# Fourier folds moved into the last LRU head, gates cut up between channel-mixing blocks, output weights and decays placed elsewhere, and chunks of k one product later, in a two-layer diffusion trunk

## The chip, the cores and the metric

The kernel runs on one core of a Trainium2 chip. The metric is the device time of one execution in microseconds. The engines are TensorE (PE; its weight loads appear as PEld), VectorE (DVE), ScalarE (ACT), GpSimd (POOL) and SyncE (SP), which issues most of the DMAs. Each engine works through its own instructions in order and waits on semaphores.

## The reference

A trunk of two layers over 1024 latent tokens and 256 context tokens of width 1024. Each layer normalises its input, shifts and scales it by a modulation that is computed from a condition, mixes, normalises again and adds the result with a gate. Layer 0 mixes with eight RG-LRU heads and four Fourier groups, layer 1 with a bidirectional retention of four heads.

```python
def fourier_branch(z, w_f):
    zg = z.astype(jnp.float32).reshape(B_, T, FNET_GROUPS, FNET_GROUP_DIM)
    f = jnp.real(jnp.fft.fft2(zg, axes=(1, 3), norm='ortho'))
    y = jnp.einsum('btgi,gij->btgj', f, w_f.astype(jnp.float32))
...
def even_mixer(...):
    xa, xb, ga, gb = jnp.split(h @ w_in, cuts, axis=-1)
    ya, yca = rglru_branch(xa, xca, ...)
    yb = fourier_branch(xb, w_f)
    y = jnp.concatenate([ya * jax.nn.silu(ga), yb * jax.nn.silu(gb)], axis=-1) @ w_out
...
def reference(...):
    for layer in range(DEPTH):
        shift, scale, gate = ada_mod(c, mod_w[layer], mod_b[layer])
        h = rms_norm(x, pre_g[layer]) * (1.0 + scale[:, None]) + shift[:, None]
        y, yc = even_mixer(...) if layer % 2 == 0 else retention_mixer(...)
        x = x + gate[:, None] * rms_norm(y, post_g[layer])
```

## The kernel before

Each fp32 product is made of three matmuls on a high and a low part of both operands (`acc3`); `split` makes the parts, the high one by a cast on ACT (or DVE), the low one by a subtraction on DVE or POOL (`low`). The 1280 tokens are worked on in chunks of 512, 512 and 256 columns. Weights pass through three raw slots of one tag, `wr`, in the pool `wp`; modulation weights (`modw`) and the DFT tables (`dr`) take the same slots.

Layer 0 runs through eight LRU heads. The head with n = 7 also makes the first Fourier inputs with `four_z(8)` and `four_z(9)` and the channel matrices of group 0. Then comes the loop over the Fourier groups g = 0 to 3. For each of the two inputs of a group the even and odd folds `ze`, `zc` are formed (by POOL for the first, by DVE for the second), combined, and split into `zx`, `zh`, `zl`. Then a gate `gate_b(2g)` is computed (24 steps of three matmuls, `pj`), then a modulation column, and then the channel mixing: six matmuls per block into `pa`, three of them with 128 contraction rows (`zh`, `zl`) and, in the even half, three with a single one (`zx`). The DFT over tokens follows (`dftmm`, tiles `pd`) for two halves ct of the group's channels, with the second gate ahead of ct = 1, and DVE and ACT combine the results into `y`, which goes to DRAM as yb_d. `mod_next` emits the column matmuls `mod_c` and the next 32-column matmuls `mod_a` of a modulation.

In group 3 the gate 7 (with the loop over k outermost, `kouter`) comes ahead of pa; then `wp` is released, and the LRU results ya_d are read back (`load_y`) while the group ends. `first_half` of the output projection then goes over the output blocks f with weights from `w1tile`; the retention's decays (`kd`, `qd`, `msk`) are computed by ACT and DVE just ahead of it, and `second_half` adds the Fourier half.

In layer 1 a `unit` makes seven (or, with the tokens as output, five) products of 24 or 48 matmuls (`pst`), and after each product takes one step of the generator `side`. For v and g that generator is `chunks_k`, which reads q and k back from DRAM (qk_d, written by the unit before), transposes k (`pkt`) and writes it out for the retention. Its two `load_qk` come at its second step and the first chunk at its third.

The order on each engine is made by a scheduler by priorities: code that is written earlier goes first, and `tc.high_priority(offset=...)` moves a piece ahead by an offset.

## Time and profile before

| | |
|---|---|
| median of three runs | 1951.94 us (1946.73 to 1958.4) |
| the profiled execution | 1954.47 us |
| its span, first to last instruction | 1952.7 us |
| mean granted TensorE clock | 0.976 |
| busy: PE, DVE, ACT, POOL | 1878.2, 1328.4, 866.8, 618.6 us |

The profile gives one execution. TensorE's granted clock has two levels, 1.00 (2.4 GHz) and 0.50 (1.2 GHz). A matmul row gives its start and its duration; as matmuls are pipelined, the pace is read from the steps between starts. The releaser in brackets is what ended the idle time ahead of a row.

### The profile page before, as it was taken

What the parts mean: (1) busy time and instruction counts of PE and PEld (TensorE: products, weight loads), DVE (VectorE), ACT (ScalarE), POOL (GpSimd) and SP (SyncE); (2) the same over time, 40 slices, a digit from 0 to 9 for tenths busy, and PEclk for the clock granted to TensorE, in tenths of its full rate; (3) what the DMA queues carried; (4) which work ended last, traced back from release to release, by engine and by line L of the source; (5) the groups of instructions that cost most, each with busy time, mean ns of one, the idle gap of its engine ahead of it and who ended that gap; (6) DMA issues with size and microseconds to landing.
All of it is one profiled execution on the core that took longest, in us unless ns stands there. A gap on an engine that the chain in (4) does not pass through costs nothing. (4 is left out here: it accounts for less than half of the span.)

```text
span 1952.7 us, 27667 instructions
## 1 busy us (share of the span) xinstructions
PE 1878.2 (96%) x10418; PEld 1578.5 (81%) x10418; DVE 1328.4 (68%) x1884; ACT 866.8 (44%) x1447; POOL 618.6 (32%) x407
## 2 busy tenths in 40 slices
PE   7999999989999899999999999999998899999997
PEld 3788888878888788888998889888896577777776
DVE  6777888742333434477678768777675887888987
ACT  5577676521222253256453332424333555454542
POOL 2411211312121241153245426253340334444544
PEclk8999999979889999999999999999999999999998
DMA  7222213213212262263872654737467555565434
GB/s 282 93 79 63 89 66 100 95 63 116 92 60 82 92 243 87 75 206 110 268 231 91 228 164 142 262 106 247 127 215 239 171 180 165 155 188 156 143 100 157
DMA packets 165110, 284.46 MB, mean 146 GB/s; under 512 B 14928, under 2 KB 94064, under 8 KB 163824
## 3 DMA queue, kind: packets, MB, share of 16 engines
q1 hardware_dynamic: 132224, 258.39, 41.1%
q10 hardware_dynamic: 32656, 24.26, 3.8%
q8 instruction: 82, 1.34, 0.3%
q14 instruction: 52, 0.43, 0.1%
q0 software_dynamic: 96, 0.04, 0.0%
HBM read 206.09 MB, written 76.55 MB: 145 GB/s over the span
## 5 line engine op out<-in xcount | busy, mean ns | idle before, releaser
L64 POOL TENSOR_TENSOR wl<-wr,wh 128x512 fp32r<-128x512 f32 (+1 forms) x80 | 153.8, 1923 | 421.4 <-ACT wh L70 396.7
L70 ACT CAST w<-wr 128x1024 fp32r<-128x1024 f32 x132 | 138.6, 1050 | 272.6 <-PE pst L59 205.3
L66 DVE TENSOR_TENSOR w<-wr,w 128x1024 fp32r<-128x1024 f32 x104 | 139.1, 1338 | 127.0 <-ACT w L70 127.0
L59 PE MATMUL pj<-xh,wl 128*128 128x512 f32 x512 | 203.0, 396 | 3.6 <-POOL wl L64 3.6
L59 PE MATMUL pj<-xh,wh 128*128 128x512 f32 x512 | 205.1, 402 | 1.0 <-ACT wh L70 0.6
L59 PE MATMUL pj<-xl,wh 128*128 128x512 f32 x512 | 202.8, 396 | 1.2 <-POOL xl L64 1.2
L59 PE MATMUL po<-xh,w 128*128 128x512 f32 x512 | 167.1, 398 | 0.0
L59 PE MATMUL pst<-xh,w 128*128 128x512 f32 x512 | 166.2, 398 | 0.5 <-DVE w L66 0.5
L64 POOL TENSOR_TENSOR w<-wr,w 128x1024 fp32r<-128x1024 f32 x28 | 70.7, 2524 | 184.3 <-ACT w L70 181.1
L59 PEld LDWEIGHTS pj<-xh,wl 128*128 128x128 f32 x512 | 97.0, 189 | 25.0 <-POOL wl L64 4.5
L59 PEld LDWEIGHTS pj<-xh,wh 128*128 128x128 f32 x512 | 96.8, 189 | 23.2 <-issue 1.4
L59 PEld LDWEIGHTS pst<-xh,w 128*128 128x128 f32 x512 | 95.9, 188 | 23.6 <-DVE w L66 1.0
L59 PEld LDWEIGHTS pj<-xl,wh 128*128 128x128 f32 x512 | 97.0, 189 | 22.1 <-POOL xl L64 2.1
L59 PEld LDWEIGHTS po<-xh,w 128*128 128x128 f32 x512 | 96.0, 188 | 22.5 <-issue 0.5
L70 ACT CAST wh<-wr 128x512 fp32r<-128x512 f32 (+1 forms) x80 | 63.4, 793 | 113.5 <-PE ph L59 49.2
L59 PE MATMUL po<-stp,qt 128*128 128x512 f32 x384 | 99.8, 404 | 7.0 <-DVE stp L66 3.4
L59 PE MATMUL pds<-vp,kh 128*128 128x512 f32 x288 | 92.5, 406 | 10.3 <-ACT kh L1152 5.5
L59 PE MATMUL po<-xl,w 128*128 128x512 f32 x256 | 101.3, 396 | 0.0
L59 PE MATMUL pst<-xl,w 128*128 128x512 f32 x256 | 101.0, 395 | 0.0
L59 PEld LDWEIGHTS po<-stp,qt 128*128 128x128 f32 x384 | 73.0, 192 | 28.5 <-DVE stp L66 6.1
L59 PE MATMUL pst<-w,xh 128*128 128x256 f32 x512 | 93.7, 285 | 0.0
L59 PE MATMUL pj<-xc,wh 128*128 128x256 f32 x512 | 91.4, 279 | 0.0
(315 smaller groups left out, 4800.8 us busy)
## 6 DMA issues: line engine op xcount, KB each, us to landing
wr<-in_w SPq DMA_DIRECT2D x72, 512.0 KB, 4.3
vp<-v_d SPq DMA_DIRECT2D x44, 512.0 KB, 4.6
wr<-in_win SPq DMA_DIRECT2D x32, 512.0 KB, 3.7
modw<-in_modw SPq DMA_DIRECT2D x32, 512.0 KB, 3.5
wr<-in_wout SPq DMA_DIRECT2D x32, 512.0 KB, 3.6
wr<-in_wout SPq DMA_DIRECT2D x56, 256.0 KB, 2.7
v_d<-st SPq DMA_DIRECT2D x48, 256.0 KB, 4.4
qt<-qs_d SPq DMA_DIRECT2D x32, 384.0 KB, 3.3
```

Of the source, the lines that this page charges most:

```text
L59: nc.tensor.matmul(o, lhsT=a, rhs=b, start=start, stop=stop)
L64: nc.gpsimd.tensor_tensor(out=o, in0=x, in1=hh, op=ALU.subtract)
L66: nc.vector.tensor_tensor(out=o, in0=x, in1=hh, op=ALU.subtract)
L70: nc.scalar.copy(h, x)
```

## The change

Six edits. (1) `mod_c`: both column matmuls first, then the reads by DVE. (2) The folds of group 0 are made in the LRU head 7, each right behind its `four_z`; the sums and casts that follow (`channel_folds`) are given a priority 40 earlier there; the DFT tables have buffers of their own (two raw ones) and a load behind the code of the head, and their high parts are cast by ACT. (3) A gate is a generator of steps, and `take` lets some of them run between two pa blocks: gate 1 in group 0, the second half of gate 2g in groups 1 and 2, gate 7 in group 3. (4) In group 3 the ya_d loads start when pa is done; the weights of the output blocks f = 0 and 1 are loaded into the tiles of the folds, and the two blocks (chunks 0 and 2) are multiplied ahead of the release of the Fourier pools (`po0`); `pd` of ct = 1 is put in the PSUM tag mm. (5) The decays become a generator that `second_half` advances. (6) `chunks_k` starts with one more empty step.

```diff
+OF0 = 40
...
             for i, part in enumerate(parts):
+                mm(c[:, 2 * i:2 * i + 2], r[:, i * P:(i + 1) * P], sel, True, True)
+            for i, part in enumerate(parts):
                 ci = c[:, 2 * i:2 * i + 2]
-                mm(ci, r[:, i * P:(i + 1) * P], sel, True, True)
                 if part == 0:
...
+    fo = pool("four_fold")
+
+    def fold(z, ct):
+
+        s2 = fo.tile([P, 2], F32, tag=f"zsp{ct}", name="zsp", bufs=1)
+        nc.vector.tensor_scalar(out=s2[:, 0:1], in0=z[:, 512:513], scalar1=1.0 / 32, scalar2=None, op0=ALU.mult)
+        nc.vector.tensor_scalar(out=s2[:, 1:2], in0=z[:, T + 129:T + 130], scalar1=1.0 / 16, scalar2=None, op0=ALU.mult)
+        t = [s2]
+        for e, op in ((0, ALU.add), (1, ALU.subtract)):
+            w = fo.tile([P, 512], F32, tag=f"ze{e}{ct}", name=f"ze{e}", bufs=1)
+            wc = fo.tile([P, P], F32, tag=f"zc{e}{ct}", name=f"zc{e}", bufs=1)
+            (nc.vector if ct else nc.gpsimd).tensor_tensor(out=w.rearrange("p (two n) -> p n two", two=2),
+                                    in0=z[:, 0:512].rearrange("p (n two) -> p n two", two=2),
+                                    in1=z[:, T:512:-1].rearrange("p (n two) -> p n two", two=2), op=op)
+            nc.vector.tensor_tensor(out=wc, in0=z[:, T + 1:T + 129], in1=z[:, NT + 1:T + 129:-1], op=op)
+            t += [w, wc]
+        return t
...
-            zf0 = four_z(8)
+            zz0 = [fold(four_z(8), 0)]
...
-        nga = gate_a(n + 1) if n < 7 else four_z(9)
+        if n < 7:
+            nga = gate_a(n + 1)
+        else:
+            zz0.append(fold(four_z(9), 1))
...
+    def channel_folds(zz, off):
+
+        with tc.high_priority(offset=off):
+            zx = [fq.tile([1, 512], F32R, tag=f"zx{p}", name=f"zx{p}") for p in "hl"]
+            split(zz[0][1][0:1, :], *zx)
+            zs = fq.tile([P, 2], F32, tag="zss", name="zss")
+            for i, (a, b) in enumerate(zip(*zz)):
+                if i == 0:
+                    nc.vector.tensor_tensor(out=zs, in0=a, in1=b, op=ALU.add)
+                else:
+                    nc.vector.tensor_tensor(out=b, in0=a, in1=b, op=ALU.add if i < 3 else ALU.subtract)
+                    if i > 2:
+                        nc.gpsimd.memset(b[0:1, :], 0.0)
+            zf = []
+            for e in range(2):
+                zh = fq.tile([P, 512], F32R, tag=f"zh{e}", name=f"zh{e}")
+                zl = fq.tile([P, 512], F32R, tag=f"zl{e}", name=f"zl{e}")
+                split(zz[1][1 + 2 * e], zh, zl)
+                zf.append((zz[1][2 + 2 * e], zh, zl))
+        return zx, zz[0][0][0:1, :], zz[0][2][0:1, :], zs, zf
...
-    dh = fc.tile([P, 2, 1028], F32R, name="dh")
-    dl = fc.tile([P, 2, 1028], F32R, name="dl")
-    COSE, COSO, SINE, SINO = (0, 258), (258, 256), (514, 256), (770, 258)
+    dr = [fc.tile([P, 514], F32, tag="dr", name="dr", bufs=2) for _ in range(4)]
+
+    dh = [[fc.tile([P, 514], F32R, name=f"dh{j}{b}") for b in range(2)] for j in range(2)]
+    dl = [[fc.tile([P, 514], F32R, name=f"dl{j}{b}") for b in range(2)] for j in range(2)]
...
+    def take(gen, n=99):
+        for _ in range(n):
+            if next(gen, 0) == 0:
+                return
...
+        def gen():
+            wh, wl = wtile(I["win"][24 + n], OW0)
+            if kouter:
+                os_ = [ps.tile([P, 512], F32, tag="mm", name="pj", bufs=4) for _ in CHUNKS]
+                for k in range(KT):
+                    for ci, (c0, cn) in enumerate(CHUNKS):
+                        acc3(os_[ci][:, :cn], wh[:, k, :], wl[:, k, :], *hx[k][ci], k == 0, k == KT - 1)
+                    yield
+            for ci, (c0, cn) in enumerate(CHUNKS):
+                if kouter:
+                    o = os_[ci]
+                else:
+                    o = ps.tile([P, 512], F32, tag="mm", name="pj", bufs=4)
+                    for k in range(KT):
+                        acc3(o[:, :cn], wh[:, k, :], wl[:, k, :], *hx[k][ci], k == 0, k == KT - 1)
+                        if k < KT - 1:
+                            yield
+                intab(nc.scalar.activation(sgb[:, c0:c0 + cn], o[:, :cn], AF.Silu))
+                yield
+
+        return sgb, gen()
...
-        for j in range(2):
-            for b in range(2):
-                s = slice(b * 514, (b + 1) * 514)
-                dr = wp.tile([P, 514], F32, tag="wr", name="dr", bufs=WRB)
-                nc.sync.dma_start(dr, I["dftc"][:, j, s])
-                split(dr, dh[:, j, s], dl[:, j, s], he="v", le="g")
-
+        for b in range(2):
+            for j in range(2):
+                raw = dr[2 * b + j]
+                nc.sync.dma_start(raw, I["dftc"][:, j, b * 514:(b + 1) * 514])
+                split(raw, dh[j][b], dl[j][b], le="g")
+
+    dft_tables()
...
+            zz = []
+            for ct in range(2):
                 z = four_z(8 + 2 * g + ct)
                 mod_next()
...
-        sgb = [gate_b(2 * g), None]
-        if not g:
-            dft_tables()
+                zz.append(fold(z, ct))
+        zx, zsx, zcx, zs, zf = channel_folds(zz, 0 if g else OF0)
+
+        sg0, gen = gate_b(2 * g)
+        take(gen, 99 if g in (0, 3) else 12)
         mod_next()
+        sgb = [sg0, None]
+        if g in (0, 3):
+            sgb[1], gen = gate_b(2 * g + 1, g == 3)
         side = iter(())
-        if g == 3:
-            sgb[1] = gate_b(7, True)
-            mod_flush()
-            wp.release()
-            lc = pool("l1c", side="right")
-            stg = pool("stage", side="right")
-            yx = [[None] * 3 for _ in range(KT)]
-            side = load_y(load_raw(ya_d, [0, 2]), yx, "g")
...
+                    take(gen, 1 if e or g == 3 else 2)
...
+        if g:
+            take(gen)
+        if g == 3:
+            mod_flush()
+            wp.release()
+            lc = pool("l1c", side="right")
+            stg = pool("stage", side="right")
+            yx = [[None] * 3 for _ in range(KT)]
+            side = load_y(load_raw(ya_d, [0, 2]), yx, "g")
+            next(side)
+
+            z = fz.tile([P, NT + 2], F32R, tag="z", name="w0", bufs=2)
+            parts = [[[fq.tile([P, 512], F32R, tag=f"z{p}{e}", name="w0") for p in "hl"] for e in range(2)],
+                     [[z[:, 512 * e:512 * (e + 1)], fz.tile([P, 512], F32R, tag=n, name="w0")] for e, n in enumerate(("cwh", "cwl"))]]
+            w0 = []
+            for f in range(2):
+                for e in range(2):
+                    raw = fo.tile([P, 512], F32, tag=f"ze{e}{f}", name="wr0", bufs=1)
+                    nc.sync.dma_start(raw, I["wout0"][f, 0, :, 4 * e:4 * e + 4, :].rearrange("p k m -> p (k m)"))
+                    split(raw, *parts[f][e], le="vg"[f])
+                w0.append(parts[f])
...
             if ct and g < 3:
-                sgb[1] = gate_b(2 * g + 1)
+                if g:
+                    sgb[1], gen = gate_b(2 * g + 1)
+                take(gen)
                 mod_next()
...
-                o = ps.tile([P, 512], F32, tag="aux", name="pd", bufs=4)
-                b0, bn = blk
+                o = ps.tile([P, 512], F32, tag="mm" if g == 3 and ct else "aux", name="pd", bufs=4)
...
+    po0 = [[], []]
+    for f in range(2):
+        for ci in (0, 2):
+            c0, cn = CHUNKS[ci]
+            o = ps.tile([P, 512], F32, tag="mm", name="po", bufs=4)
+            for k in range(KT):
+                acc3(o[:, :cn], *[w0[f][k // 4][p][:, k % 4 * P:(k % 4 + 1) * P] for p in range(2)], *yx[k][ci], k == 0, k == KT - 1)
+            po0[f].append((c0, cn, o))
...
+    def decays():
+
+        mskE = stage(512).rearrange("p (a n) -> p a n", n=P)
+        nc.sync.dma_start(mskE, I["mskE"])
+        nc.sync.dma_start(lg, I["lg"].partition_broadcast(P))
+        nc.sync.dma_start(kx, I["kx"])
...
-            for c0, cn, o in outproj0(f, 0, yx, chunks, f == KT - 1):
+            for c0, cn, o in outproj0(f, 0, yx, chunks, f == KT - 1) if f > 1 or 1 in chunks else po0[f]:
...
-    steps(second_half([0, 2]), 99)
+    dec = decays()
+    for _ in second_half([0, 2]):
+        next(dec, None)
+    steps(dec, 99)
...
     def chunks_k(h):
+        yield
         yield
         xs = [load_qk(h, 0), load_qk(h, 1)]
```

On SP, at the end of head 7 and the start of group 0 (`dr`: DFT tables, `wr`: weights of a gate, `modw`: modulation weights, `ya_d`: the store of an LRU head's result, `cd`: for the channel matrices). Before:

```order
L544 DMA dr<-in_dftc 128x514 [waits DMAHW7_49,DMAHW5_49,Pool_49]
L544 DMA dr<-in_dftc 128x514 [waits DMAHW1_49,PE_49]
L544 DMA dr<-in_dftc 128x514 [waits DMAHW2_49,PE_49]
L544 DMA dr<-in_dftc 128x514 [waits DMAHW7_49,Pool_49]
L175 DMA modw<-in_modw 128x1024 [waits DMAHW0_49,Pool_49]
L175 DMA modw<-in_modw 128x1024 [waits DMAHW1_49,Pool_49]
L242 DMA wr<-in_win 128x1024 [waits DMAHW6_49,DMAHW2_49,Pool_49]
L485 DMA ya_d<-sga 128x1280 [waits DVE_49]
```

After:

```order
L176 DMA modw<-in_modw 128x1024 [waits DMAHW7_49,DMAHW5_49,Pool_49]
L176 DMA modw<-in_modw 128x1024 [waits DMAHW1_49,PE_49]
L244 DMA wr<-in_win 128x1024 [waits DMAHW2_49,PE_49]
L176 DMA modw<-in_modw 128x1024 [waits DMAHW1_49,Pool_49]
L508 DMA ya_d<-sga 128x1280 [waits DVE_49]
L176 DMA modw<-in_modw 128x1024 [waits DMAHW7_49,DMAHW4_49,PE_49]
L390 DMA cd<-in_cd 128x512 [waits DMAHW0_49,PE_49]
L627 DMA dr<-in_dftc 128x514 x2
L627 DMA dr<-in_dftc 128x514 [waits DMAHW7_49,Pool_49]
L627 DMA dr<-in_dftc 128x514 [waits DMAHW2_49,DMAHW0_49,Pool_49]
```

The gate's load moved ahead of the last head's store, and the tables moved behind it and behind two more loads.

On TensorE, at the start of the channel mixing of group 1 (`pj`: steps of gate 2, `zxh` and `zxl`: the one-row parts). Before:

```order
L59 MATMUL pa<-cwh,zh_3950 128x256
L59 MATMUL pa<-cwl,zh_3950 128x256
L59 MATMUL pa<-cwh,zl_3951 128x256
L59 MATMUL pa<-cwh,zxh 128x256
L59 MATMUL pa<-cwl,zxh 128x256
L59 MATMUL pa<-cwh,zxl 128x256
L59 MATMUL pa<-cwh,zh_3950 128x256
L59 MATMUL pa<-cwl,zh_3950 128x256
L59 MATMUL pa<-cwh,zl_3951 128x256
L59 MATMUL pa<-cwh,zxh 128x256
L59 MATMUL pa<-cwl,zxh 128x256
L59 MATMUL pa<-cwh,zxl 128x256
```

After:

```order
L60 MATMUL pa<-cwh,zh_3959 128x256
L60 MATMUL pa<-cwl,zh_3959 128x256
L60 MATMUL pa<-cwh,zl_3960 128x256
L60 MATMUL pa<-cwh,zxh 128x256
L60 MATMUL pa<-cwl,zxh 128x256
L60 MATMUL pa<-cwh,zxl 128x256
L60 MATMUL pj<-xh_127,wh 128x512
L60 MATMUL pj<-xl_128,wh 128x512
L60 MATMUL pj<-xh_127,wl 128x512
L60 MATMUL pj<-xh_132,wh 128x512
L60 MATMUL pj<-xl_133,wh 128x512
L60 MATMUL pj<-xh_132,wl 128x512
```

Between two blocks of six pa matmuls there are now six of the gate.

On SP, in group 3 (`in_wout`: weights of the output projection, `in_win`: those of gate 7, `ya_d`, `yb_d`: LRU and Fourier results). Before, at the first reads of ya_d, and at the first loads of output weights:

```order
L242 DMA wr<-in_win 128x1024 [waits DMAHW3_49,Pool_49]
L509 DMA st<-ya_d 128x512 [waits DMAHW2_49,DMAHW6_49,PE_49,Pool_49]
L505 DMA st<-ya_d 128x2x256 [waits DMAHW0_49,PE_49]
L509 DMA st<-ya_d 128x512 x2
L505 DMA st<-ya_d 128x2x256
L509 DMA st<-ya_d 128x512 [waits DMAHW4_49]
L509 DMA st<-ya_d 128x512 [waits DMAHW5_49]
```

```order
L509 DMA st<-ya_d 128x512 [waits DMAHW2_49]
L705 DMA wr_5853<-in_wout 128x1024 [waits DMAHW3_49,DVE_49,PE_49]
L705 DMA wr_5923<-in_wout 128x1024 [waits DMAHW4_49,PE_49]
L724 DMA st<-in_mskE 128x512 [waits DMAHW5_49,Pool_49]
L726 DMA lg<-in_lg 128x8 [waits DMAHW6_49,DVE_49]
L728 DMA kx<-in_kx 128x8 [waits DMAHW7_49]
L682 DMA yb_d<-y 128x1280 [waits DMAHW0_49,DVE_49]
L705 DMA wr_6133<-in_wout 128x1024 [waits DMAHW4_49,DMAHW1_49,Pool_49]
L705 DMA wr_6191<-in_wout 128x1024 [waits DMAHW3_49,DMAHW2_49,DVE_49]
L682 DMA yb_d<-y 128x1280 [waits DVE_49]
```

After, at the same two places:

```order
L244 DMA wr<-in_win 128x1024 [waits DMAHW3_49,Pool_49]
L692 DMA wr_5568<-in_wout 128x512 [waits DVE_49]
L692 DMA wr_5572<-in_wout 128x512 [waits DMAHW0_49,DVE_49]
L692 DMA wr_5576<-in_wout 128x512 [waits DVE_49]
L692 DMA wr_5580<-in_wout 128x512 [waits DMAHW2_49,DVE_49]
L531 DMA st<-ya_d 128x512 [waits DMAHW5_49,PE_49]
L527 DMA st<-ya_d 128x2x256 [waits DMAHW4_49,PE_49,Pool_49]
L531 DMA st<-ya_d 128x512
```

```order
L755 DMA yb_d<-y 128x1280 [waits DMAHW7_49,DVE_49]
L531 DMA st<-ya_d 128x512 [waits DMAHW0_49,Pool_49]
L531 DMA st<-yb_d 128x512 [waits DMAHW1_49,Pool_49]
L527 DMA st<-yb_d 128x2x256 [waits DMAHW2_49]
L787 DMA wr_5956<-in_wout 128x1024 [waits DMAHW3_49,PE_49]
L787 DMA wr_6026<-in_wout 128x1024 [waits DMAHW4_49,PE_49]
```

The early weights, in four pieces, now stand ahead of the reads of ya_d, and the load of the next block's weights behind the second store to yb_d and the first reads of it.

## Rows read from the trace of the kernel before

**Rows 1.** The profile page: busy time, share of the span, instructions of each engine.
```profile
PE 1878.2 (96%) x10418; PEld 1578.5 (81%) x10418; DVE 1328.4 (68%) x1884; ACT 866.8 (44%) x1447; POOL 618.6 (32%) x407
```

**Rows 2.** Timeline of TensorE (start us, us, engine, line, operation): the same matmul at either clock.
```profile
379.67 0.39 PE L59 MATMUL pj<-xh,wh 128*128 128x512 f32 x1
...
382.42 0.39 PE L59 MATMUL pj<-xh,wh 128*128 128x512 f32 x1
...
396.90 0.63 PE L59 MATMUL pj<-xh,wh 128*128 128x512 f32 x1
...
398.18 0.63 PE L59 MATMUL pj<-xh,wh 128*128 128x512 f32 x1
```

**Rows 3.** The same timeline, TensorE's waits in Fourier group 0 (idle before, releaser in brackets).
```profile
389.09 0.50 PE L59 MATMUL pj<-xh,wh 128*128 128x512 f32 x1 [0.60 <-ACT wh L70]
...
392.17 0.50 PE L59 MATMUL pj<-xh,wl 128*128 128x512 f32 x1 [2.34 <-POOL wl L64]
395.88 0.58 PE L59 MATMUL pa<-cwh,zh 128*128 128x256 f32 x1 [3.21 <-ACT zh L70]
```

**Rows 4.** Timelines of SP, ScalarE and GpSimd (POOL) ahead of the same place.
```profile
354.80 18.07 SPq L544 DMA_DIRECT2D dr<-in_dftc  x4
...
384.43 0.33 SPq L242 DMA_DIRECT2D wr<-in_win  x1
387.31 0.33 SPq L485 DMA_DIRECT2D ya_d<-sga  x1
...
387.99 1.05 ACT L70 CAST wh<-wr 128x1024 fp32r<-128x1024 f32 x1 [13.93 <-DMA wr<-in_win]
...
392.08 2.55 POOL L564 TENSOR_TENSOR ze<-z 128x512 f32<-128x512 f32 x2
```

**Rows 5.** Stretches: us; busy (instructions) of PE, PEld, DVE, ACT, POOL; clock; DMA share; GB/s.
```profile
395.88:412.00 16.12, 16.12 (x52) 12.65 (x52) 5.01 (x11) 3.71 (x7) 0.66 (x2) 0.50 0.06 25
412.00:416.95 4.95, 4.95 (x22) 4.75 (x23) 1.67 (x5) 0.64 (x2) 0.00 (x0) 0.50 0.00 0
488.00:492.04 4.04, 4.04 (x24) 2.99 (x23) 0.84 (x2) 0.59 (x1) 0.00 (x0) 1.00 0.60 195
492.04:502.28 10.24, 10.24 (x36) 8.46 (x37) 2.30 (x5) 4.08 (x8) 2.36 (x1) 0.50 0.17 53
573.96:584.20 10.24, 10.24 (x41) 9.20 (x41) 3.03 (x7) 3.35 (x7) 2.38 (x1) 0.50 0.17 51
669.53:672.94 3.41, 3.41 (x17) 3.20 (x15) 2.32 (x5) 2.76 (x6) 2.56 (x2) 0.50 1.05 377
679.77:686.60 6.83, 4.03 (x17) 3.61 (x17) 6.29 (x16) 3.22 (x7) 2.31 (x2) 0.50 0.23 86
739.00:770.00 31.00, 31.00 (x177) 26.85 (x176) 15.54 (x29) 11.20 (x19) 5.15 (x2) 1.00 0.32 103
1098.68:1103.03 4.35, 4.35 (x20) 4.35 (x21) 4.35 (x7) 0.86 (x3) 0.62 (x1) 0.50 0.32 85
```

**Rows 6.** Timeline of TensorE, one-row matmuls; then TensorE's waits (total us, times, longest).
```profile
488.15 0.38 PE L59 MATMUL pa<-cwh,zxh 1*128 1x256 f32 x1
...
PE pkt L59 <- DMA st<-qk_d: 5.9, 3, 4.7
PE mod_c L59 <- DVE sh L187: 1.6, 3, 0.6
```

**Rows 7.** Timelines of TensorE, SP and POOL in the last Fourier group.
```profile
679.13 0.39 PE L59 MATMUL pd<-dh,ah 128*128 128x258 f32 x1 [2.19 <-DVE spe L655]
...
683.09 0.55 PE L59 MATMUL pd<-dh,ah 128*128 128x256 f32 x1 [2.80 <-DVE y L671]
...
663.36 0.38 SPq L505 DMA_DIRECT2D st<-ya_d  x1
...
676.48 3.98 POOL L64 TENSOR_TENSOR xl<-st,xh 128x512 fp32r<-128x512 f32 x3 [0.49 <-ACT xh L70]
```

**Rows 8.** Timeline of TensorE at the first chunk of k.
```profile
1098.68 1.20 PE L59 MATMUL pkt<-st 128*128 128x128 f32 x4 [4.74 <-DMA st<-qk_d]
```

More of the change, by code (lines that the diff above doesn't have):

```diff
@@ L486, in _build @@
         sga = nga
-    zs0 = [zf0, nga]
     if "ya" in dbg:
@@ L527, in _build, with ftile @@
     fp = pool("four_out")
-    fq = pool("four_in")
+    first = {}
+    def ftile(shape, dt, tag, bufs=1):
+        if tag in first:
+            return first.pop(tag)
+        return fp.tile(shape, dt, tag=tag, name=tag, bufs=bufs)
+    LOW = (("nb", 4, 2), ("ac0", 256, 1), ("ac1", 256, 1), ("y", NT, 1), ("spe", 258, 1), ("u", 256, 1), ("sqe", 256, 1), ("v", 256, 1))
+    first.update({n: fp.tile([P, w], F32, tag=n, name=n, bufs=b) for n, w, b in LOW})
+    first.update({f"a{p}{e}{par}": fp.tile([P, 2, 256], F32R, tag=f"a{p}{e}{par}", name=f"a{p}", bufs=1)
+                  for e in range(2) for par in range(2) for p in "hl"})
@@ L581, in _build @@
-        zf = []
-        for e in range(2):
-            zh = fq.tile([P, 512], F32R, tag=f"zh{e}", name=f"zh{e}")
-            zl = fq.tile([P, 512], F32R, tag=f"zl{e}", name=f"zl{e}")
-            split(zz[1][1 + 2 * e], zh, zl)
-            zf.append((zz[1][2 + 2 * e], zh, zl))
-        sgb = [gate_b(2 * g), None]
-        if not g:
-            dft_tables()
+                zz.append(fold(z, ct))
+        zx, zsx, zcx, zs, zf = channel_folds(zz, 0 if g else OF0)
+        sg0, gen = gate_b(2 * g)
@@ L611, in _build @@
                         acc3(pa[:, j, :], zx[0][:, s], zx[1][:, s], ch[0:1, 1, :], cl[0:1, 1, :], False, True)
-                ah = fp.tile([P, 2, 256], F32R, tag=f"ah{e}{par}", name="ah")
-                al = fp.tile([P, 2, 256], F32R, tag=f"al{e}{par}", name="al")
+                    take(gen, 1 if e or g == 3 else 2)
+                ah, al = [ftile([P, 2, 256], F32R, f"a{p}{e}{par}") for p in "hl"]
                 split(pa, ah, al)
                 A[e, par] = (ah, al)
-                next(side, None)
             pa = ps.tile([P, 2, 256], F32, tag="aux", name="pac", bufs=4)
@@ L629, in _build @@
             mm(pn[:, 0:2], cf[0:1, 1, cs], zsx, False, True)
-            nb = fp.tile([P, 4], F32, tag="nb", name="nb", bufs=2)
+            nb = ftile([P, 4], F32, "nb", 2)
             nc.vector.tensor_copy(nb[:, 0:2], pn[:, 0:2])
@@ L663, in _build @@
             nc.vector.tensor_tensor(out=x, in0=sqe, in1=qo[:, 0:256], op=ALU.subtract)
-            y = fp.tile([P, NT], F32, tag="y", name="y", bufs=1)
+            y = ftile([P, NT], F32, "y")
             L = TC
@@ L1104, in chunks_k @@
     def chunks_k(h):
+        yield
         yield
```

91 lines of the change are left out of this document (31 added, 60 removed).

## The prediction

> **What bounds the kernel now.** I read the shares of busy time first: TensorE is busy for 96% of the span [rows 1], so no other engine sets the time as a whole, and a change can win in only two ways, by closing a gap in which TensorE waits or by undoing a stretch in which its granted clock stands at the lower of its two levels (0.50, that is 1.2 instead of 2.4 GHz). To price the second I compared the same matmul at both levels [rows 2]: between 379.67 and 382.42 there are twelve 512-column matmuls, 0.229 us each; between 396.90 and 398.18 there are three, 0.427 us each. A busy microsecond at the lower level therefore does what 0.534 us do at the upper, and 0.466 us of it are lost. Then I went through TensorE's order for its waits and through the table by stretches for the clock. Four places have both, and the change touches them all: the first Fourier group (388 to 417 us), the pa blocks of groups 1 and 2 (from 492 and 574), the last group (669 to 687), and the first chunk of k (1094 to 1103).
>
> **Folds in the last LRU head (g = 0).** Now TensorE waits 0.60 us for the cast wh, 2.34 for POOL's wl and 3.21 for zh [rows 3], 6.15 together, and works on at the lower clock for 16.12 + 4.95 = 21.07 us [rows 5]; 21.07 x 0.466 = 9.8. The cause stands in the other queues [rows 4]: the four dr loads hold the weight slots and their issue takes 18.07 us, so gate 1's weights are issued only at 384.43, cast at 387.99, and POOL does their low part before the fold of z8, which starts at 392.08 although z8 is old. In the new order gate 1's load stands ahead of the tables, the folds stand on POOL ahead of that low part, and the casts of zh follow in the last head. All three waits lose their cause: ceiling 6.15 + 9.8 = 15.95.
> What is late next is the DFT tables. On SP their loads now stand behind the store of head 7's ya_d, which goes out at 387.31 [rows 4] when DVE has finished the head, and behind a modulation load. With two buffers, the second pair also waits for POOL's dl of the first. TensorE wants the first table after pa and 12 of gate 1's steps. The pa work is 16.12 x 0.534 = 8.6, less 0.9 for four gate matmuls that lie in it, so near 8; a step of three 512-column matmuls is 0.69, twelve are 8.2. From 388.5 that is 405. A load took 3.56 us from issue to cast (384.43 to 387.99 [rows 4]). Loads issued at about 390 give the first pair by 396, the second after ACT's cast and POOL's low part at 402 to 407. So the stall is between 0 and 3 us; I take 1.5, since the first pair has time and only the second is near. The casts now sit on ACT, which waits there in order; behind them are pa's ah casts, and that is the way in which late tables would hurt earlier than 405. Term: **-14.5**.
>
> **Half of gate 2g between pa blocks (g = 1, 2).** At 488 to 492.04 TensorE is busy for 4.04 of 4.04 us at the full clock, and then the clock falls for 10.24 us, all busy; at 573.96 the same [rows 5]. What TensorE did before is a run of pa blocks in which half of the matmuls have a single contraction row (1x256, [rows 6]); so the clock fell without any idle time, after work that uses one row of the array. In the new order two gate steps, six full matmuls, follow each block of the first kind (the order shows it), which brings these one-row matmuls from half of the time to a quarter or a third. The added cost is none: the same matmuls, one PSUM tile longer in use. Bounds: nothing gained, or both stretches, 2 x 10.24 x 0.466 = 9.5; I take the latter, as 12 gate steps also stand ahead of the modulation matmuls. Term: **-9.5**.
> The Trainium skill (TensorE: Matmul & The Clock Gate, section "Why this matters for your kernels") names idle gaps between bursts of matmuls as what makes the throughput drop in the middle of a kernel. By that rule alone nothing would be gained here, as there is no gap to close; the rows speak against it, since they show the fall with TensorE busy throughout, and by it the sum would be 9.5 us smaller (the second rival).
>
> **mod_c.** Both column matmuls before their reads: the wait on DVE's sh, 1.6 us in three places [rows 6], has no cause left; DVE and TensorE do the same work. Term: **-1.6**.
>
> **The last group (g = 3) and two early blocks.** Now there are gaps of 2.19 and 2.80 us at the second half's pd [rows 7], and 3.41 + 4.03 busy us at the lower clock [rows 5], 7.44 x 0.466 = 3.5; ceiling 8.5. The gate between pa blocks, pd tiles in the other PSUM tag (so that they don't wait for DVE's reads) and early weights for f = 0, 1 take away each cause. What is late next: the ya_d loads started at 663.36 [rows 7], when gate 7 was done and pa was still to come. Now gate 7 ends with pa, some 7 us later, so they start near 670. POOL's low parts take 3.98/3 = 1.33 us each [rows 7], eight of them 10.6, and two low parts of the early weights stand ahead. The last x low comes near 685 to 687, while TensorE reaches po0 at about 678 (an estimate: pa's end near 670, then twice 24 pd matmuls of half a 512-column one, 2.8 us, with their small ones) and needs one k in 0.7 us. That costs 2 to 3 us in small pieces. Next, the load of f = 2's weights now waits for TensorE's last pd and stands on SP behind the last y's store and the first loads of yb; 3.56 us to its cast and POOL's low part put it within 0 to 3 us of being late. So the term lies between -8.5 and +1 (all of this late and the clock falling once more); I take -5. Term: **-5**.
>
> **Decays.** The exponentials move to second_half, where ACT is busy for 11.20 of 31.00 us [rows 5], so ACT's idle time hides them; without that cover they would delay the acc copies that free PSUM, by at most their few us. Term: **0**.
>
> **Chunks of k.** Waits for the qk_d reload are 5.9 us in three places [rows 6], the longest 4.74 [rows 8], after it 4.35 us at the lower clock [rows 5], 2.0. One product of 48 matmuls of 256 columns at 0.115 (half of 0.229), 5.5 us, now stands in between, so the data that came at 1098.68 are there when they are asked for, at 1099.2. The reload of the third chunk moves behind one more weight load; it is wanted a product later too. The eight chunks still end within the last unit. Ceiling 7.9; I leave 0.5 for the bare margin. Term: **-7.4**.
>
> **Sum.** -14.5 - 9.5 - 1.6 - 5 - 7.4 = -38.0. The profiled run took 1954.47 us, so it would take 1916.5; the median of the runs shown, 1951.94, lies 2.5 lower, which gives **1914** for a median.
>
> **Rivals.**
> 1. *Late tables.* For: the slack in group 0 is a microsecond at most, on three queues. Against: the first pair has several. The second pair late by 4 us and a clock stretch as at 492 (4.8) cost some 9 more than the 1.5 taken: 1922. Chance 0.12.
> 2. *The clock falls at pa as before.* The order changes, but the thing that it is meant to change doesn't: the one-row matmuls still come in blocks. For: that the fall is tied to them is read from two places only. Against: with six full matmuls after each block there is no run left like the one ahead of 492. 1914 + 9.5 = 1923.5. Chance 0.12.
> 3. *The last group gives back its gain.* ya_d, xl and f = 2's weights late, a gap over 2 us and a fall as at 679.77: 5 to 6 us lost: 1920. For: the loads start 7 us later. Against: 8 us of early weights that wait for nothing. Chance 0.12.
> 4. *Slower than before: the mixture itself keeps the clock down.* At 395.88 to 412, pa mixed with gate matmuls, the clock stayed low throughout [rows 5]. If the clock stays down wherever pa blocks and gate steps alternate, the mixed stretches run low from end to end: four times 8 us of pa and 8.2 + 5.6 + 5.6 + 13.9 of gate steps, 65 us at full clock, cost 65 x 0.873 = 57 more, less 9.8 + 9.5 + 1.6 that are lost there already, against some 17 us of other gains: 36 - 17 = +19, 1971. It decides from about 44 of the 65 us at the lower clock (38 / 0.873). Against: the clock there had fallen in a gap of 3.21 us, and only four gate matmuls were mixed in. Chance 0.05.
> The forecast has 0.55; two of the first three together (1930 to 1938) 0.04.
>
> **The range.** From 1900 (all ceilings: 15.95 + 9.5 + 1.6 + 8.5 + 7.9 = 43.5, so 1908 for a median, and 1903 if it falls as low as the lowest run shown stands under its median, 5 us; 3 more for what the sum doesn't see) to 1934 (the first three rivals, half of what two of them together give, and the spread of the runs). A measurement can tell about 0.5% from no change, 10 us. All cases but the fourth rival gain more than that unless several terms fail together: faster 0.90, same 0.04, slower 0.06.
>
> **What would show it.** In the new profile: no TensorE wait for wh, wl or zh ahead of the first pa, and the clock at 1.00 from there to the end of group 0; a wait of pd for dl or dh there is the first rival. Clock 1.00 through the pa of groups 1 and 2, or a stretch of 10.24 us at 0.50 as before. No wait on sh. After the last pa, waits of po on xl or w show the third. No wait of pkt on the reload. I am wrong altogether if a wait opens that the old trace doesn't hold, most likely where TensorE now meets the tables or f = 2's weights.

## The result and the profile after

| | before | after |
|---|---|---|
| median | 1949.74 us (4 runs) | 1924.78 us (4 runs, 1919.62 to 1925.78) |
| ratio | | 0.9868, interval 0.9843 to 0.9894 |
| profiled execution | 1954.47 us | 1925.78 us |
| mean granted clock | 0.976 | 0.989 |

The change wins 25 us in the medians (1.3%) and 28.7 between the profiled executions, against 38.0 forecast for the latter. TensorE is busy 25.5 us less for the same 10418 matmuls [rows 1]. The page's busy line:

```profile
PE 1852.7 (96%) x10418; PEld 1558.6 (81%) x10418; DVE 1323.4 (69%) x1881; ACT 866.1 (45%) x1453; POOL 620.9 (32%) x408
```

TensorE's waits of the changed kernel from 380 to 700 us (total us, times, longest):

```profile
PE po L60 <- ACT w L71: 4.4, 1, 4.4
PE po L60 <- ACT sqe L732: 3.7, 1, 3.7
PE pj L60 <- POOL wl L65: 1.3, 1, 1.3
PE pd L60 <- DVE al L67: 1.2, 1, 1.2
PE po L60 <- POOL xl L65: 0.3, 1, 0.3
```

The waits of [rows 3] on wh and zh are gone, as are those of [rows 7] on spe and y; in their place po, the early blocks of the output projection, waits for sqe (ACT's copy of a `pd`; only then is the PSUM tile free) and then for f = 2's weights. The same columns as in [rows 5], group 0, groups 1 and 2, and the two stretches of the last group at the lower clock:

```profile
388.00:412.00 24.00, 22.80 (x146) 18.75 (x138) 10.05 (x21) 9.53 (x20) 5.20 (x6) 1.00 0.31 105
480.00:520.00 40.00, 40.00 (x252) 34.81 (x251) 17.13 (x39) 9.18 (x19) 8.93 (x5) 1.00 0.32 106
560.00:600.00 40.00, 40.00 (x242) 34.41 (x241) 14.97 (x31) 9.29 (x19) 7.56 (x4) 1.00 0.31 105
655.56:658.97 3.41, 3.22 (x8) 2.54 (x9) 3.41 (x6) 1.95 (x5) 3.41 (x3) 0.50 0.13 52
679.45:682.86 3.41, 3.41 (x10) 2.65 (x10) 1.99 (x2) 3.28 (x5) 1.90 (x1) 0.50 0.67 205
```

Where 492.04 and 573.96 of [rows 5] stood at 0.50, the clock is now 1.00. And far behind every edit, in the first unit of layer 1, a wait has opened that the old trace doesn't hold:

```profile
1020.28 1.22 PE L60 MATMUL pst<-xh,w 128*128 128x512 f32 x2 [5.64 <-DVE w L67]
```

To place the gain, each matmul of one trace was set against the same matmul of the other. What the time ahead of before grows by, stage by stage (profiled executions):

| place | forecast | measured |
|---|---|---|
| start to 380 us | | -0.1 |
| group 0 | -14.5 | -14.9 |
| mod_c | -1.6 | -1.1 |
| groups 1 and 2 | -9.5 | -10.7 |
| last group, early blocks | -5 | +3.7 |
| clock at 922 us (3.41 us at 0.50 before, none now) | | -1.5 |
| unit at 1014 us | | +7.7 |
| first chunk of k | -7.4 | -7.6 |
| behind it, to the end | | -4.2 |
| sum | -38.0 | -28.7 |

Two places miss, by 8.7 and 7.7 us; 7 us are won beyond the forecast, most of them in places that it didn't name. Two rows are less than they seem. The stretch at 922 us stands in the same place of the program again in experiments 2, 7, 8 and 10 (from 901.27 us in the second), so its 1.5 us are probably chance and no gain of the change. And the unit at 1014 us and the first chunk of k hang together: without the edit of `chunks_k` (experiment 2), 5.9 of the 7.6 us come at the first chunk all the same, because the wait at 1014 has by then made TensorE late.

Single executions differ by up to 6 us in the first 60 us alone, where TensorE's wait for modr is 4.7 to 5.6 us in most and 1.27, 0.23 or nothing in three, so the experiments are read by such stages and not by their total.

### The profile page after: what moved, and what is told of

Its sections match the earlier page's. It is cut to its first block, busy times and chain, and to the rows that moved or that the text cites. A ratio compares the mean times of both kernels' runs of the same rounds, so it can differ in the third digit from the quotient of the medians.

```text
span 1924.0 us, 27696 instructions
## 1 busy us (share of the span) xinstructions
PE 1852.7 (96%) x10418; PEld 1558.6 (81%) x10418; DVE 1323.4 (69%) x1881; ACT 866.1 (45%) x1453; POOL 620.9 (32%) x408
## 5 line engine op out<-in xcount | busy, mean ns | idle before, releaser
L71 ACT CAST w<-wr 128x1024 fp32r<-128x1024 f32 (+1 forms) x134 | 138.9, 1038 | 279.2 <-PE pst L60 211.7
L67 DVE TENSOR_TENSOR w<-wr,w 128x1024 fp32r<-128x1024 f32 (+1 forms) x105 | 142.2, 1355 | 134.1 <-ACT w L71 124.2
L65 POOL TENSOR_TENSOR w<-wr,w 128x1024 fp32r<-128x1024 f32 (+1 forms) x29 | 73.6, 2541 | 214.8 <-ACT w L71 211.5
L60 PE MATMUL pds<-vp,kh 128*128 128x512 f32 x288 | 93.7, 409 | 13.8 <-ACT kh L1241 10.7
L60 PE MATMUL pst<-t,w 128*128 128x512 f32 x368 | 91.6, 397 | 0.0
```

What stands on the lines that cost most here:

```text
L60: nc.tensor.matmul(o, lhsT=a, rhs=b, start=start, stop=stop)
L65: nc.gpsimd.tensor_tensor(out=o, in0=x, in1=hh, op=ALU.subtract)
L67: nc.vector.tensor_tensor(out=o, in0=x, in1=hh, op=ALU.subtract)
L71: nc.scalar.copy(h, x)
```

## The experiments

**1. The slots of the output weights.** `w1tile` deals out slots in the pools wa and wb in turn; the two early blocks leave out two calls, so all later weights sit two slots further. This run puts the turn back.

```diff
-    turn = [0, 0]
+    turn = [2, 0]
```

> The changed kernel, with the counter that picks the weight slots of w1tile started at 2 instead of 0; nothing else. Theory: the two early output blocks (po0) call w1tile twice less, so every later weight tile sits in the other pair of slots, and layer 1's first unit finds another slot free first; that put its weight low parts behind others on DVE and made the 5.65 us wait of pst on DVE w at 1014 with 6.8 us at the lower clock. Then this kernel shows no wait over 1 us there, and everything behind it comes 7 to 8 us earlier: near 1918 us in one run. Rival: the wait comes from the extra empty step of the chunks of k; then it stays at 5 to 6 us and the time stays near 1925.

1920.56 us. At 1014 us 7.75 us come back, and 1.8 are lost again at 1075 (`pst` waits 1.41 for DVE's w); by the end 5.2 remain. So the shifted slots made the new wait. How is seen on POOL and DVE. The changed kernel, POOL and then DVE:

```profile
1006.67 2.40 POOL L1136 TENSOR_TENSOR wr<-wr,wr 128x1024 f32<-128x1024 f32 x1 [11.96 <-PE pst L60]
1009.14 2.73 POOL L1137 TENSOR_TENSOR wr<-wr,wr 128x1024 f32<-128x1024 f32 x1
1011.83 3.38 POOL L1139 TENSOR_TENSOR wr<-wr,wr 128x1024 f32<-128x1024 f32 x1
...
1010.19 2.77 DVE L67 TENSOR_TENSOR w<-wr,w 128x1024 fp32r<-128x1024 f32 x1 [0.57 <-ACT w L71]
1012.88 2.88 DVE L67 TENSOR_TENSOR st<-st 128x512 fp32r<-128x512 f32 x1
...
1019.01 2.35 DVE L67 TENSOR_TENSOR w<-wr,w 128x1024 fp32r<-128x1024 f32 x2
```

The first experiment's DVE:

```profile
1007.42 1.23 DVE L67 TENSOR_TENSOR w<-wr,w 128x1024 fp32r<-128x1024 f32 x1 [0.33 <-ACT w L71]
```

With the shifted slots POOL adds up the weights of the next product early, while DVE makes low parts; a low part then takes 2.77 instead of 1.23 us, and the one that TensorE wants is reached only at 1019.01. Of the theory's 7 to 8 us behind it, 5.2 are left.

**2. Without the step in chunks_k.**

```diff
     def chunks_k(h):
         yield
-        yield
```

> The changed kernel without the extra empty step of the chunks of k. Theory (slots): the wait at 1014 stays, 5 to 6 us, and the stall of pkt on the reload of qk_d comes back, 4.7 us and 2 us of clock at the first chunk and about 1 us more at later ones: 7 to 8 us slower than the changed kernel, near 1933. Rival (the step made the wait at 1014): that wait is gone, the stall is back, and the time is about the same as the changed kernel, 1925.

1932.88 us. The wait at 1014 stays (5.67), so the step doesn't cause it. But `pkt` then waits only 0.80 us for the reload, where before it was 4.74 [rows 8]:

```profile
1081.23 0.68 PE L60 MATMUL pkt<-st 128*128 128x128 f32 x4 [0.80 <-DMA st<-qk_d]
```

TensorE has already lost that time at 1014. Against the kernel before, this run wins 5.9 us at the first chunk without the step. 7.5 us are lost against the changed kernel, of them 3.1 between 640 and 930 us, by clock stretches in places that the edit doesn't touch. 1.7 are lost at the first chunk, 1.3 more by 1450 us, and the rest behind it.

**3. The splits of ya behind both y chains.**

```diff
             def dftmm(e, par, blk):
-                next(side, None)
```

> The changed kernel, with the steps that read ya_d back and split it in the last Fourier group written behind the two halves' y instead of between the pd products. Theory: in the changed kernel DVE did the x casts and lows of chunk 0 ahead of the first y, so its tiles came free late; po0 waited 3.68 us for a PSUM tile, and the weights of block f = 2, behind the store of the second y on SP, came 4.35 us late. Here y comes first: the wait of po0 falls under 1 us, the store of the second y goes out 6 to 9 us earlier, the wait for f = 2's weights falls under 1.5 us, no fall of the clock between 650 and 690; 8 to 11 us faster, near 1916. Rival: f = 2's weights wait for memory that the early blocks hold, not for the store; then the 3.68 go and the 4.35 stay or grow by as much, and the time is 1922 to 1926.

1923.76 us; the last group wins 0.9 us. The wait for sqe falls from 3.68 to 1.73, but four waits of 0.32 to 0.68 us for POOL's x lows come, and f = 2's weights still cost 3.09. The theory failed: the second store of y goes out at 668.04, where it was 668.65. As it hardly moved, this run doesn't tell whether f = 2's weights wait for the store or for memory.

**4. No gate steps between pa blocks (groups 0 to 2).**

```diff
-        take(gen, 99 if g in (0, 3) else 12)
+        take(gen)
...
-                    take(gen, 1 if e or g == 3 else 2)
+                    take(gen, 1 if g == 3 else 0)
```

> The changed kernel, with no gate steps between the pa blocks of groups 0, 1 and 2: gate 2g whole ahead of pa, gate 1 whole ahead of the second half. Theory (runs of one-row matmuls bring the clock down): the clock falls again in pa of groups 1 and 2, 10.24 us at 0.50 each, 4.8 us slower for each, and in group 0 too, though no gap precedes it: 9 to 15 us slower, 1935 to 1940. Rival (only gaps bring it down): no fall in any of the three groups, and the time stays within 2 us of the changed kernel.

1936.40 us, 10.0 lost over the three groups. Stretches ahead of a fall and behind it, in groups 0 and 2; in group 1 the clock falls at 478.46, for 3.41 us:

```profile
389.00:393.13 4.13, 4.13 (x24) 3.08 (x23) 3.36 (x5) 1.28 (x1) 0.00 (x0) 1.00 0.14 58
393.13:399.96 6.83, 6.83 (x18) 4.77 (x18) 0.75 (x2) 3.65 (x8) 1.15 (x1) 0.50 0.74 253
...
549.50:553.56 4.06, 4.06 (x39) 3.18 (x38) 0.76 (x3) 0.97 (x2) 0.00 (x0) 1.00 0.40 128
553.56:567.21 13.65, 13.65 (x51) 11.27 (x50) 3.60 (x8) 4.08 (x8) 2.36 (x1) 0.50 0.11 39
```

TensorE is busy throughout ahead of both falls; ahead of the first, 12 of its 24 matmuls have one row. Group 0 falls too (393.13), so there also it is the mixture that holds the clock, besides the absent wait. The prediction read the same from two places of the kernel before; the stretch ahead of the second, which [rows 5] doesn't show:

```profile
569.86:573.96 4.10, 4.10 (x22) 2.98 (x22) 0.80 (x2) 1.32 (x3) 0.00 (x0) 1.00 0.43 128
```

But busy isn't full pace here. In the fourth experiment the starts step by 0.12 us within a triple of equal rows, and by 0.20 to 0.23 around each change between 128 rows and one:

```profile
389.65 0.39 PE L60 MATMUL pa<-cwh,zh 128*128 128x256 f32 x1
389.87 0.28 PE L60 MATMUL pa<-cwl,zh 128*128 128x256 f32 x1
389.99 0.28 PE L60 MATMUL pa<-cwh,zl 128*128 128x256 f32 x1
390.20 0.38 PE L60 MATMUL pa<-cwh,zxh 1*128 1x256 f32 x1
390.43 0.28 PE L60 MATMUL pa<-cwl,zxh 1*128 1x256 f32 x1
```

**8. The same without one-row matmuls in groups 1 and 2.** Their term of the channel sum is left out; group 0 keeps it.

```diff
-                    acc3(pa[:, j, :], zh[:, s], zl[:, s], ch[:, e, :], cl[:, e, :], True, e == 1)
-                    if e == 0:
+                    acc3(pa[:, j, :], zh[:, s], zl[:, s], ch[:, e, :], cl[:, e, :], True, e == 1 or g in (1, 2))
+                    if e == 0 and g not in (1, 2):
```

> The changed kernel with pa unmixed in the groups 0, 1 and 2, as in the fourth experiment, and the one-row matmuls left out in the groups 1 and 2 (their term of the channel sum is missing from the output); group 0 keeps them and is the control. If runs of one-row matmuls bring the clock down: a stretch at 0.50 near 393 as in the fourth experiment, none near 478 and none near 554; against the fourth experiment -7 us of clock and about -2.8 us of matmuls not done, 1926 to 1928. If the small matmuls as such (256 columns, many operand changes) do it, the stretches of 3.41 and 13.65 us stay and the time is 1933 to 1935.

1922.14 us, lower than either theory's time, mostly since the start was one of the short ones (6.4 us against the fourth). The stretches decide; pa runs from 466 to 471 us in group 1 and from 539 to 544 in group 2:

```profile
388.03:391.44 3.41, 3.41 (x12) 2.93 (x12) 0.69 (x1) 0.53 (x2) 0.00 (x0) 0.50 0.96 338
466.00:486.00 20.00, 20.00 (x132) 17.14 (x124) 8.56 (x22) 5.98 (x13) 2.39 (x1) 1.00 0.28 99
542.00:562.00 20.00, 20.00 (x120) 17.61 (x119) 7.38 (x20) 5.41 (x12) 2.40 (x1) 1.00 0.19 71
```

Group 0 falls, groups 1 and 2 don't, though pa is a single run there. So it is the blocks with one-row matmuls, in a run, that bring the clock down, and the mixture helps by thinning them out. What of them does it is not separated: with the one-row matmuls, the slower steps around them are gone too, and the even half of pa takes about 1.5 us instead of 4.4:

```profile
466.80 0.28 PE L60 MATMUL pa<-cwh,zl 128*128 128x256 f32 x1
466.92 0.28 PE L60 MATMUL pa<-cwh,zh 128*128 128x256 f32 x1
```

**5. The last group as before.** Gate 7 whole, ya_d behind it, `pd` in one tag, no early weights and no po0.

```diff
         if g in (0, 3):
             sgb[1], gen = gate_b(2 * g + 1, g == 3)
         side = iter(())
+        if g == 3:
+            take(gen)
+            mod_flush()
...
+            side = load_y(load_raw(ya_d, [0, 2]), yx, "g")
...
-            for c0, cn, o in outproj0(f, 0, yx, chunks, f == KT - 1) if f > 1 or 1 in chunks else po0[f]:
+            for c0, cn, o in outproj0(f, 0, yx, chunks, f == KT - 1):
```

> The changed kernel with the last Fourier group as it was before: gate 7 whole ahead of pa, the loads of ya_d behind gate 7, pd always in the same PSUM tag, no early weights and no early blocks po0, so that the slots of the output weights turn as before too. Theory (the last group lost 3.7 us instead of winning 5, and the turned slots cost 7.7 at 1014 us, of which the first experiment gave back 5 to 6): no wait of po for sqe at 652, none of pst for w at 1014; about -3.7 and -5.5 against the changed kernel, 1914 to 1918. Rival (the last group's change is worth something and the wait at 1014 comes from elsewhere, for instance from what runs ahead of it): TensorE waits of 2.2 and 2.8 us at the second half's pd come back, the wait at 1014 stays: 1928 to 1931.

1936.95 us median of 5, ratio to before 0.9954 (0.9935 to 0.9973). My theory fell: the last group is 19 us longer than in the changed kernel, not 3.7 shorter, and pd waits for DVE again (2.3 and 3.7 us), as the rival said. The rest of it holds: the wait at 1014 is gone (-7.7). TensorE and SP at the end of the group:

```profile
677.64 0.79 PE L60 MATMUL po<-xh,w 128*128 128x512 f32 x1 [16.33 <-ACT w L71]
```

```profile
668.69 0.32 SPq L745 DMA_DIRECT2D yb_d<-y  x1
669.11 0.39 SPq L527 DMA_DIRECT2D st<-yb_d  x1
669.58 1.44 SPq L531 DMA_DIRECT2D st<-yb_d  x2
671.11 1.87 SPq L769 DMA_DIRECT2D wr<-in_wout  x4
```

In the kernel before, the first weights were asked for at 672.27, ahead of both stores of y (684.89 and 693.67); here they stand behind the second store (668.69) and behind the first loads of yb. The folds' pool now lies beneath those of the DFT, so the tiles of wa and wb come to lie on tiles that live until the last pd; that this is why the load comes late is read from the code, not shown. So most of what the early blocks give is cover: they hide, for two of the blocks, a delay that came with the other edits.

**9. A third early block, and the turn put back.** f = 2's weights get places of their own (raw parts in the two dead buffers of the DFT tables and three other dead tiles, casts into the folds' tiles).

```diff
-            for f in range(2):
+            for f in range(3):
                 for e in range(2):
-                    raw = fo.tile([P, 512], F32, tag=f"ze{e}{f}", name="wr0", bufs=1)
+                    raw = rd[2 * f + e]()
...
-    turn = [0, 0]
+    turn = [3, 0]
...
-            o = ps.tile([P, 512], F32, tag="mm", name="po", bufs=4)
+            o = ps.tile([P, 512], F32, tag="aux" if f == 2 else "mm", name="po", bufs=4)
```

> The changed kernel with a third early block: f = 2's output weights have a place of their own too (loaded into the two raw buffers of the DFT tables and three other dead tiles, cast into the tiles of the folds), its matmuls go into the other PSUM tag, and the slots of the later output weights turn as before the change. Theory: the wait of 4.35 us for f = 2's cast and the stretch at 0.50 behind it go (-6), f = 3's weights, issued about when f = 2's were (671.6), are cast by 681 and wanted at 683; the wait of 5.64 at 1014 goes and about 2 to 2.5 us of what it hid come back (-5.2 in the first experiment); the 3.68 us at 652 stay. 1911 to 1916. Rival: SP's queue and POOL are the limit in the last group, so f = 3's weights are late in f = 2's place: 1918 to 1921.

1910.79 us median of 5 (1908.86 to 1913.66), ratio to before 0.9806 (0.979 to 0.9822): faster than both kernels (0.9806 against 0.9868 for the changed one). The last group wins 7.1 us, the unit at 1014 a net 5.1. TensorE's largest wait left in the group, and the stretch where f = 2's and f = 3's weights were wanted:

```profile
653.52 0.77 PE L60 MATMUL po<-xh,w 128*128 128x512 f32 x1 [3.08 <-DVE y L748]
```

```profile
670.00:690.00 20.00, 20.00 (x123) 17.77 (x122) 5.57 (x2) 8.32 (x12) 12.21 (x8) 1.00 0.92 330
```

**10. The same with the rest of the last group as before** (the loads of ya_d too, which the cut leaves out).

```diff
+        if g == 3:
+            take(gen)
...
-                o = ps.tile([P, 512], F32, tag="mm" if g == 3 and ct else "aux", name="pd", bufs=4)
+                o = ps.tile([P, 512], F32, tag="aux", name="pd", bufs=4)
```

> The kernel of the ninth experiment with the rest of the last group as before the change: gate 7 whole ahead of pa, the loads of ya_d behind it, pd always in the same PSUM tag. The early weights cover what delayed po by 16.33 us in the fifth experiment, so this one weighs gate 7 in pieces and the second PSUM tag by themselves. If they are worth what the prediction said: waits of 2.3 and 3.7 us at the second half's pd and more clock at 0.50 (6.83 to 17 us were seen between 637 and 664 in the fifth), less the 3.68 us at 652 that go: 3 to 8 us longer than the ninth, 1915 to 1923. If they only moved the wait from pd to po: within 1.5 us of the ninth.

1920.15 us median of 4, ratio to before 0.9851 (0.9835 to 0.9867), against 0.9806: 9.4 us longer in the medians, 5.3 of them in the last group by the traces. TensorE there:

```profile
648.50 0.39 PE L60 MATMUL pd<-dh,ah 128*128 128x256 f32 x1 [1.34 <-DVE al L67]
...
661.42 0.55 PE L60 MATMUL pd<-dh,ah 128*128 128x256 f32 x1 [3.28 <-DVE nb L708]
...
686.58 0.73 PE L60 MATMUL po<-xh,w 128*128 128x512 f32 x2 [1.03 <-POOL w L65]
```

With pa in one run again, the clock falls in this group too with TensorE busy, as it did at 669.53 in the kernel before [rows 5]:

```profile
636.50:640.78 4.28, 4.28 (x23) 2.80 (x21) 1.92 (x3) 2.21 (x4) 0.66 (x1) 1.00 0.90 290
640.78:644.19 3.41, 3.41 (x15) 3.30 (x15) 3.41 (x7) 2.54 (x5) 2.54 (x3) 0.50 0.95 279
```

So gate 7 in pieces and the second tag for pd, with the ya_d loads behind pa, are worth about 5 us once the weights are in time.

**11. The ninth with ya behind both y chains**, as in the third.

> The kernel of the ninth experiment with the splits of ya behind both y chains, as in the third experiment. There the wait for sqe went from 3.68 to 1.73 us, but 1.8 us of small waits for x lows came, and the wait for f = 2's weights hid part of the rest. If the chain of y on DVE, queued behind the casts of ya, is what holds po's PSUM tile, the 3.08 us at 650 fall to about 1.5 and 1 to 2 us are won: 1909 to 1910. If POOL's low parts of x (1.3 us each) are the pace of the first early block in any case, the waits only change their name: 1910 to 1912.

1916.31 us median of 5, ratio 0.9832 (0.9812 to 0.9852): no gain, and longer than either theory said. The last group is 1 us longer than in the ninth; 1.73 us for sqe and five waits of 0.3 to 0.7, four of them for POOL's x lows, stand in place of one of 3.08, so the waits change their name as the rival said. The rest of the difference lies outside the group, at the start and behind 1070 us, and its cause was not separated.

**6. The kernel before with the later chunks of k alone.**

```diff
     def chunks_k(h):
+        yield
         yield
```

> The kernel before with the later chunks of k alone. By the prediction's term -7.4 us: no wait of pkt for the reload, no clock stretch at 1096. If what the reload's wait hid is late next (DVE and POOL lag between 1000 and 1100 us, as the changed kernel's wait at 1014 suggests), only 3 to 5 us are won and new waits for the low parts or casts of k stand in the same heads.

1942.94 us, one execution. From 1080 to 1120 us it wins 5.3 us: `pkt` no longer waits and the stretch at 1096 is gone, but

```profile
1097.29 0.38 PE L59 MATMUL pst<-w,t 128*128 128x256 f32 x1 [1.41 <-DVE w L66]
```

takes its place. By 1600 us it is 9 us ahead of where it stood at 1080; the later chunks and the start of the retention give the rest, in steps of a microsecond whose causes I did not separate.

**7. mod_c with each product followed by its read, as before.**

```diff
-                mm(c[:, 2 * i:2 * i + 2], r[:, i * P:(i + 1) * P], sel, True, True)
-            for i, part in enumerate(parts):
                 ci = c[:, 2 * i:2 * i + 2]
+                mm(ci, r[:, i * P:(i + 1) * P], sel, True, True)
```

> The changed kernel with the two column products of the modulation each followed by its read, as before. By the prediction's term 1.6 us are lost again, in three places of about 0.5 on DVE's sh, all after 400 us; if the order of these products also made the new wait of 1.54 us at 71.66 (for ACT's xa), that one goes and the sum is 0 to -0.5 us: 1925 to 1926.5 either way, so the places decide, not the time.

1937.40 us, one execution, although its start was 5 us shorter. Counted from there, not 1.6 but 12 us are lost by 500 us, 9.0 of them in group 0 and 3.0 at the next columns. Some 5 more are lost behind 500 us, 2.2 of them between 640 and 930; their causes were not separated. The wait in group 0, and the clock behind it:

```profile
386.07 0.38 PE L60 MATMUL mod_c<-sel,modr 128*128 128x2 f32 x2 [3.24 <-DVE sh L188]
```

```profile
387.77:401.43 13.66, 13.66 (x39) 10.57 (x39) 0.69 (x1) 2.50 (x6) 2.62 (x4) 0.50 0.47 150
```

DVE now has the folds in its queue there, so its read of the column is late; TensorE waits for it between two tiny matmuls and the clock falls right after.

## Why the prediction was right, and where it was wrong

1914 was forecast, 1924.78 came; the range (1900 to 1934) and the direction hold.

- *Folds in the last LRU head: right in size* (-14.5, measured -14.9). None of the three waits is left and the clock is 1.00. The cost was not the DFT tables (no wait for dh or dl; rival 1 did not come) but 1.20 us for DVE's al. That the sum came out is partly luck, since the 1.5 us stood for another wait. The new wait can cost more: in the fifth experiment it was 1.39 us, and 3.41 us at 0.50 followed (401.71 to 405.12). And the step took mod_c for a separate term: the seventh experiment shows that the folds would have lost 9.0 of their 14.9 us with the old order of mod_c.
- *Gates between pa: right* (-9.5, measured -10.7). Experiments 4 and 8 show the mechanism as the prediction had it, as far as runs of blocks with one-row matmuls go. Its "after work that uses one row of the array" is one reading of it; the slower steps between the starts are another, and no run separates them. The Trainium skill (TensorE: Matmul & The Clock Gate, section "Why this matters for your kernels") names idle gaps between bursts of matmuls as what brings the throughput down; here the clock fell at 393.13 and 553.56 with TensorE busy for 4.13 of 4.13 and 4.06 of 4.06 us, so such gaps are not the only cause, and the measurement decides. Rival 2 did not come, nor rival 4: the mixed stretches run at 1.00.
- *mod_c: right by its own waits* (-1.1), and wrong as an account of what it is worth in the changed kernel (12).
- *The last group: wrong* (-5, measured +3.7); rival 3, which I had given 0.12, came, though of its three causes only the weights counted (xl cost 0.3 us, the reads of ya_d nothing). The failing step is "3.56 us to its cast and POOL's low part put it within 0 to 3 us of being late". The order on SP was as forecast: the load of f = 2's weights was issued at 671.61, behind the store of y at 668.65. But its cast came 6.52 us after that (678.13), with three more weight loads issued behind it within 2.2 us, and po waited 4.35 us with the clock low behind it. While it ran, the DMA engines were busy for 94% of the time, against 46% under the load of [rows 4]; that the other transfers made it slow is likely, but no run tests it. After, and before:

```profile
671.61:678.13 6.52, 3.27 (x26) 3.01 (x24) 0.00 (x0) 1.11 (x2) 6.52 (x6) 1.00 0.94 300
```

```profile
384.43:387.99 3.56, 3.56 (x50) 3.50 (x53) 3.53 (x9) 0.00 (x1) 0.00 (x0) 1.00 0.46 152
```

The second failing step was that pd's other tag would remove the waits on DVE; it moved them, to a wait of po for sqe (3.68), and when the casts of ya no longer stood ahead of y on DVE (experiment 3), that wait was 1.73. Experiment 10 shows that the gate in pieces and the tag are worth about 5, but the 5 of the forecast stood for the whole group, with the weights at 0 to 3 us late in it. With the weights in time (experiment 9) the group is 7.1 us shorter than in the changed kernel, and so 3.4 shorter than before.
- *Decays: right* (0); from 690 to 900 us nothing moves.
- *Chunks of k: the wait and the clock stretch go as forecast; that the size fits (-7.4, measured -7.6) is luck.* Experiment 6 gives 5.3 there alone: in the kernel before, a late low part is next (1.41 us), which the term had not priced. The same 1.41 us stands in the first experiment, without the wait at 1014, and not in the changed kernel. There most of the 7.6 us are owed to that wait: by experiment 2 the step itself is worth 1.7 at the first chunk. So the 7.7 lost at 1014 and the 7.6 won here largely cancel, and part of what is lost at 1014 was due a little later anyway. Behind the first chunk, some 4 us more are won than the term held (in experiment 6 too).
- *What the sum did not hold:* the wait at 1014. I followed the weights of f = 2 only to the end of the group, not the counter that every later slot hangs on. That is "a wait that the old trace doesn't hold", in a place that I hadn't named.
- *Slips in the working:* the rows give 0.537 (0.2292 to 0.4267 us), not 0.534, and 1093.94 + 5.5 is 1099.4, not 1099.2; neither moves a term by more than 0.3 us.

With two places mended, f = 2's weights and the wait at 1014 (experiment 9), the kernel takes 1910.79 us, 3 us below the forecast.

## What to carry to other kernels

When an edit drops or adds a call that deals out buffers in turn, follow the counter to the end of the program: the order of work hundreds of microseconds later hangs on it. When a step is moved ahead, ask which small read on the same engine now stands behind it and who waits for that read, since a wait of 3 us cost 9. And ask of each edit whether it gains or only covers: the early blocks mostly covered a delay that came with the other edits, for without them TensorE stood still for 16.33 us.

## What the runs showed of the hardware

- *Runs of blocks with one-row matmuls bring the clock down with no idle time in the trace.* In the fourth experiment 4.13 us at full clock and fully busy, half of the matmuls 1x256, were followed by 6.83 us at 0.50; with the one-row matmuls left out, 20.00 of 20.00 us at 1.00 in the places where groups 1 and 2 had fallen. Over all traces, the clock fell during or right behind each of the twelve unmixed pa runs with one-row matmuls that began at 1.00 (kernel before, experiments 4, 5, 6, 8 and 10), and behind no mixed one without a wait of TensorE in between. Whether it is the one row or the slower steps around it (0.20 to 0.23 us instead of 0.12) is open.
- *DVE and POOL slow each other down.* A 128x1024 low part on DVE took 1.23 us with POOL idle and 2.77 beside POOL's sum; that sum, 2.40 us undisturbed, took 2.73 and 3.38. The Trainium skill (SBUF — State Buffer, section "Who interferes with whom") says that a DVE instruction with both inputs in SBUF contends with a GpSimd instruction that reads SBUF and that the second one blocks; the trace agrees: the low part that starts at 1010.19 ends 1.09 us behind the end of POOL's sum (1011.87), nearly its own 1.23; POOL's next sum ends 2.25 us behind that, nearly its own 2.40. Such waits stand in DVE's queue ahead of the low part for which TensorE waits 5.64 us.
- *The same wait at the start has two sizes.* `mod_c` at 28 us waited 5.61 us for modr in one execution, 0.23 and 1.27 in two others of code that is the same up to there but for mod_c's order in one of them. With it the first 60 us differ by up to 6 us, so medians of a few executions may differ for that alone. The changed kernel, the seventh and the eighth experiment:

```profile
34.39 1.02 PE L60 MATMUL mod_c<-sel,modr 128*128 128x2 f32 x4 [5.61 <-DVE modr L180]
```

```profile
29.30 0.38 PE L60 MATMUL mod_c<-sel,modr 128*128 128x2 f32 x2 [1.27 <-DVE modr L180]
```

```profile
29.43 0.61 PE L60 MATMUL mod_c<-sel,modr 128*128 128x2 f32 x4 [0.23 <-DVE modr L180]
```
